# Two layers of a hybrid trunk on one core: gate slabs, turned norm factors, ada folds and two small operations put elsewhere

## The chip, the core and the metric

The program runs on one core of a Trainium2 chip. The core has engines that run side by side, each through its own list of instructions in order: TensorE (PE in the profile: matrix products and transpositions into PSUM), VectorE (DVE), ScalarE (ACT) and GpSimd (POOL) for elementwise work, and SyncE (SP), which issues the loads and stores. An instruction whose operands are not ready holds up all that stand behind it on its engine. The metric is the device time of one execution in microseconds; lower is better.

## The reference

Two layers over 512 latent tokens (x) and 256 context tokens (ctx), 1024 channels, float32. The second layer ("last") needs of the context only keys and values. Per layer, cut to what matters:

```python
mx = silu(c) @ w_ada + b_ada            # "ada rows": 6 shifts, scales and gates; mc likewise from c_ctx
hx = rmsnorm(x, norm1_g) * (1 + ax1) + sx1
p  = hx @ w_in                          # columns: conv GLU (a, g) | q | k | v | merge gates
z  = a * sigmoid(g);  y_conv = silu(layernorm(depthwise_conv31(z))) @ w_conv_out
q, k = rope(rmsnorm(q)), rope(rmsnorm(k))
w  = softmax(q0 k0') - lam * softmax(q1 k1')     # 8 heads, two maps each
o  = rmsnorm(w @ v) * (1 - lam_init);   y_attn = o @ w_attn_out
x += gx1 * ((g_conv * y_conv + g_attn * y_attn) @ w_out)
x += gx2 * relu(rmsnorm(x, norm2_g) * (1 + ax2) + sx2 @ w_mlp1)**2 @ w_mlp2
```

The hidden layer of the last line has 4096 channels. The output is x.

## The kernel before

Activations stand channel by channel: 128 channels on the partitions, 8 groups of channels, tokens along the free dimension. X holds the residual stream of 768 tokens (latent 0 to 511, context 512 to 767).

Each float32 product is made of three: every operand is a high part plus a low part, and TensorE does high x high (L109), high x low (L110), low x high (L111). Weights come as slabs of 1024 x 256 (`load_slab`): a load on SP into a "raw" buffer, then in two halves of 128 x 1024 the high part by a ScalarE copy (L76) and the low part by a subtraction (L77) on VectorE or GpSimd. A state entry "behind" makes the two steps of a slab be issued after a named instruction, "turn" does so for the second half alone. The order on each engine is set once, when the program is built, by a scheduler that simulates it; within a layer the steps run as generators which are merged by given costs.

A layer goes through these stages.

- Norm 1 in groups of 256 tokens (`norm_mod`): squares on ScalarE are summed by VectorE into acc (L354), TensorE sums over channels (nc_n, L327), VectorE scales (ms_n), GpSimd raises to -1/2, VectorE multiplies the identity by each factor (dg_n, L312), TensorE spreads the factors (nb_n, L316), and VectorE, ScalarE and GpSimd make the high and low parts (h1h and h1l, for norm 2 h2h and h2l). In the first layer's feed-forward part the norm of the second layer runs with the last additions to X, and the second layer's first q/k slab (wqk) and value slab (wv) are made ready there (`v_first`).
- Attention, head by head: q and k are normed and turned by GpSimd's rotary work (rqk, rw, ra, rb, dup) and transposed (qkT). Scores S, weights e, their transpositions wT with parts wth and wtl, outputs av, copied out by ScalarE (uo). The factor of each head's norm is gathered in rsall. During the last head the conv projections run: ca, then cg, whose sigmoid sg (L510) multiplies z.
- Mixing: the 31 taps of the depthwise convolution on VectorE (cacc, L963), spread over TensorE's gate products gt (slabs wg, half 1 for attention, half 0 for the convolution, four each), the turned factors (`spill_rstd`: rsT, L818, stored and loaded back spread over partitions as arb), the products of attention outputs with them (ar, L990), then ya (attention branch; its operand's parts are named h1l too), the layer norm of the convolution (tot, ln), yc (convolution branch) and the output projection o.
- Feed-forward in four chunks of 1024 hidden channels: f, then r, which is added to X (L1158). Meanwhile the first layer computes the second one's ada rows (`ada_rows`): 48 loads of half slabs, ScalarE and VectorE multiply and add (adaac, L276, L279), every second one is transposed and reduced into a column of adp (L289, L290), and after every 16 a TensorE product folds the partitions (adaps, L252). One step is taken behind each block of hidden channels (`ada_step`); what is left is drained ahead of the last chunk's r.

## Time and profile before

| what | us |
|---|---|
| median of 3 runs | 2350.78 (2348.27 to 2351.1) |
| the profiled execution | 2350.59, span 2348.8 |
| TensorE busy | 2275.5 |
| VectorE, ScalarE, GpSimd busy | 1491.8, 997.2, 685.5 |
| mean granted TensorE clock | 0.991 |

A row of the timeline gives the start, the time from the start of the first to the end of the last of its instructions, engine, line, operation, output and inputs, size and count; in brackets the idle time of the engine before it and what ended that. A row of the list of waits gives the total, the number of times and the longest. Windows show the busy time of each engine in a stretch and the clock that TensorE was granted there.

### The profile page before, as it was taken

How to read it: one execution, taken by the hardware profiler on the slowest of the kernel's cores; microseconds unless marked ns; L12 is line 12 of the kernel's file. 1: busy time of each engine (PE TensorE's matmuls, PEld its weight loads, DVE VectorE, ACT ScalarE, POOL GpSimd, SP SyncE). 2: the span in 40 equal slices, each digit the busy share in tenths (PEclk: the TensorE clock that was granted, in tenths of full speed). 3: DMA queues.
4: the chain of work that ended last, by engine and by line, in shares of the span. 5: the costliest groups of instructions: out<-in, count | busy, mean ns of one | idle time of the engine just before them, and what ended most of it. 6: DMA issues, size and time to landing. Idle time of an engine off the chain costs nothing.

```text
span 2348.8 us, 36385 instructions
## 1 busy us (share of the span) xinstructions
PE 2275.5 (97%) x14626; PEld 2039.2 (87%) x14626; DVE 1491.8 (64%) x2587; ACT 997.2 (42%) x1965; POOL 685.5 (29%) x790
## 2 busy tenths in 40 slices
PE   8999999999999999999999998999999999999999
PEld 6999998888878988888888998999877779888887
DVE  6777776699657455565656467767759966433332
ACT  5556654522333353342514345655642334432432
POOL 1866754100000133232323266757610000000000
PEclk9999999999999999999999999999999999999999
DMA  9211111143535123434343311111114324223222
GB/s 315 58 44 30 45 44 45 46 160 126 180 117 167 59 81 110 133 110 133 108 135 112 105 46 57 44 44 44 61 59 141 112 90 126 90 90 100 98 90 72
DMA packets 222570, 224.76 MB, mean 96 GB/s; under 512 B 6256, under 2 KB 212544, under 8 KB 222272
## 3 DMA queue, kind: packets, MB, share of 16 engines
q1 hardware_dynamic: 222400, 222.43, 29.5%
q8 instruction: 115, 1.88, 0.3%
q14 instruction: 55, 0.45, 0.1%
HBM read 208.73 MB, written 13.67 MB: 95 GB/s over the span
## 4 chain that ended last, share of the span: by engine, by line
PE 81%; DVE 9%; POOL 4%; ACT 3%; DMA 2%; issue 1%; ACTq 0%; SPq 0%; POOLq 0%; DVEq 0%
PE r L109 6%; PE r L111 6%; PE r L110 6%; PE f L110 6%; PE f L109 6%; PE f L111 6%; PE gt L109 3%; PE gt L111 3%; PE gt L110 3%; PE qk L109 2%; PE qk L110 2%; PE qk L111 2%; PE o L109 2%; PE o L110 2%; PE o L111 2%
## 5 line engine op out<-in xcount | busy, mean ns | idle before, releaser
L110 PE MATMUL f<-h2l,h_w 128*128 128x512 f32 (+1 forms) x832 | 284.6, 343 | 1.3 <-POOL h2l L77 1.3
L109 PE MATMUL f<-h2h,h_w 128*128 128x512 f32 (+1 forms) x832 | 282.8, 343 | 2.2 <-ACT h2h L76 1.7
L109 PE MATMUL r<-fh,h_w 128*128 128x512 f32 (+1 forms) x832 | 282.9, 341 | 0.0
L111 PE MATMUL f<-h2h,l_w 128*128 128x512 f32 (+1 forms) x832 | 282.9, 342 | 0.0
L110 PE MATMUL r<-fl,h_w 128*128 128x512 f32 (+1 forms) x832 | 282.9, 340 | 0.0
L111 PE MATMUL r<-fh,l_w 128*128 128x512 f32 (+1 forms) x832 | 282.8, 340 | 0.0
L77 POOL TENSOR_TENSOR l_w<-r_w,h_w 128x1024 fp32r<-128x1024 f32 x64 | 156.9, 2473 | 340.0 <-ACT h_w L76 340.0
L76 ACT ACTIVATE h_w<-r_w 128x1024 fp32r<-128x1024 f32 x128 | 128.6, 1052 | 255.9 <-PE r L110 117.2
L963 DVE SCALAR_TENSOR_TENSOR cacc<-z,cols,cacc 128x783 f32<-128x783 f32 (+1 forms) x240 | 201.4, 889 | 0.4
L279 DVE SCALAR_TENSOR_TENSOR adaac<-ar,cvec,adaac 128x256 f32<-128x256 f32 x336 | 164.9, 553 | 42.8 <-DMA ar<-in_w_ada_dram 23.0
L1158 DVE SCALAR_TENSOR_TENSOR X<-r,ad,X 128x512 f32<-128x512 f32 (+1 forms) x104 | 65.1, 626 | 189.8 <-PE r L111 189.4
L109 PE MATMUL qk<-h_wqk,h1h 128*128 128x256 f32 x640 | 182.6, 288 | 2.1 <-ACT rw L558 1.1
L110 PE MATMUL qk<-l_wqk,h1h 128*128 128x256 f32 x640 | 180.1, 284 | 0.0
L111 PE MATMUL qk<-h_wqk,h1l 128*128 128x256 f32 x640 | 176.3, 284 | 0.2 <-POOL h1l L77 0.2
L110 PEld LDWEIGHTS f<-h2l,h_w 128*128 128x128 f32 x832 | 159.0, 191 | 20.2 <-POOL h2l L77 2.4
L109 PEld LDWEIGHTS f<-h2h,h_w 128*128 128x128 f32 x832 | 158.1, 191 | 20.9 <-ACT h2h L76 2.3
L111 PEld LDWEIGHTS f<-h2h,l_w 128*128 128x128 f32 x832 | 158.8, 191 | 17.6
L111 PEld LDWEIGHTS r<-fh,l_w 128*128 128x128 f32 x832 | 157.7, 190 | 17.7
L110 PEld LDWEIGHTS r<-fl,h_w 128*128 128x128 f32 x832 | 157.8, 190 | 17.4
L109 PEld LDWEIGHTS r<-fh,h_w 128*128 128x128 f32 x832 | 157.7, 190 | 17.3
L730 DVE TENSOR_REDUCE st<-S 128x1 f32<-128x768 f32 (+1 forms) x160 | 134.4, 845 | 57.4 <-PE S L728 56.1
L1239 DVE TENSOR_TENSOR fl<-fr,fh 128x512 fp32r<-128x512 f32 (+1 forms) x104 | 71.0, 688 | 132.4 <-ACT fr L1238 132.1
(255 smaller groups left out, 6298.0 us busy)
## 6 DMA issues: line engine op xcount, KB each, us to landing
r_w<-in_w_mlp_dram SPq DMA_DIRECT2D x64, 1024.0 KB, 5.3
ada<-in_w_ada_dram SPq DMA_DIRECT2D x24, 1024.0 KB, 5.5
ar<-in_w_ada_dram SPq DMA_DIRECT2D x48, 512.0 KB, 3.6
r_wqk<-in_w_in_dram SPq DMA_DIRECT2D x32, 512.0 KB, 5.1
r_wg<-in_w_in_dram SPq DMA_DIRECT2D x16, 1024.0 KB, 5.8
r_wv<-in_w_in_dram SPq DMA_DIRECT2D x8, 1024.0 KB, 5.3
r_wao<-in_w_attn_out_dram SPq DMA_DIRECT2D x8, 1024.0 KB, 4.8
r_wo<-in_w_out_dram SPq DMA_DIRECT2D x8, 1024.0 KB, 8.8
```

Source lines behind the costliest of these rows:

```text
L76: nc.scalar.activation(out=hi, in_=src, func=AF.Copy)
L77: return (lo_eng or nc.vector).tensor_tensor(out=lo, in0=src, in1=f32(hi), op=ALU.subtract)
L109: nc.tensor.matmul(ps, sh, mh, start=first, stop=False)
L110: nc.tensor.matmul(ps, sh, ml, start=False, stop=False)
L111: nc.tensor.matmul(ps, sl, mh, start=False, stop=last)
L279: nc.vector.scalar_tensor_tensor(out=a[:, q], in0=r[:, j], scalar=cvec[:, k, q : q + 1], in1=a[:, q], op0=ALU.mult, op1=ALU.add)
L730: nc.vector.tensor_reduce(out=st[:, m : m + 1], in_=S[:, :nkey], axis=AX.X, op=ALU.max, negate=True)
L963: nc.vector.scalar_tensor_tensor(out=ca[cc][:, :CV], in0=zt[cc][:, t : t + CV], scalar=wcol, in1=ca[cc][:, :CV], op0=ALU.mult, op1=ALU.add)
L1158: state["done"] = nc.vector.scalar_tensor_tensor(out=X[:, mb, g], in0=ps[:, :W], scalar=gate[:, s, mb : mb + 1], in1=X[:, mb, g], op0=ALU. ...
L1239: state["done"] = nc.vector.tensor_tensor(out=fl[mb][:, g], in0=r[:, :W], in1=f32(fh[mb][:, g]), op=ALU.subtract).ins
```

## The change

It does four things.

1. `ada_rows` yields once more before each fold, so that a fold and all that comes after it are taken one step later.
2. `rstd_bcast` can multiply the identity on ScalarE. Norm 2 of the first layer does so for tokens 256 to 511.
3. In both layers the first gate slab (half 1, slab 0) is split behind the sigmoid of the conv gate block that was issued last before it. The second gate slab (1, 1) is taken after the last head's merge and split behind the last head's copy uo. The turned factors (`spill_rstd`) are taken after the issue of slab (1, 2), in a PSUM buffer of another pool.
4. The second half of layer 1's first value slab is issued behind the last sum of squares instead of behind the last low part of the norm, and its low part is made by VectorE, the first half's still by GpSimd.

```diff
@@ -291,6 +291,7 @@
                     out=part[:, :, 4 * (s % 8) : 4 * (s % 8) + 4].rearrange("p c n -> p n c"),
                     in_=b.rearrange("p (n c r) -> p n c r", n=4, c=4), axis=AX.X, op=ALU.add)
                 if s % 8 == 7:
+                    yield
                     fold(s - 7)
 
     def ada_gain(L, which, ks=slice(0, KT)):
@@ -302,21 +303,24 @@
                 op0=ALU.add, op1=ALU.mult)
 
 
-    def rstd_bcast(colsum, n, scale, name):
+    def rstd_bcast(colsum, n, scale, name, scalar=False):
 
         ms = spool.tile([P, 8], F32, tag="ms", name=f"ms_{name}")
         nc.vector.tensor_scalar(ms[:, :n], colsum, scale, EPS, ALU.mult, ALU.add)
         nc.gpsimd.tensor_tensor(out=ms[:, :n], in0=ms[:, :n], in1=mhalf[:, :n], op=ALU.pow)
         dg = spool.tile([P, 4, P], F32, tag="dg", name=f"dg_{name}", bufs=1)
         for t in range(n):
-            nc.vector.tensor_scalar(dg[:, t, :], ident, ms[:, t : t + 1], None, ALU.mult)
+            if scalar:
+                nc.scalar.activation(out=dg[:, t, :], in_=ident, func=AF.Copy, scale=ms[:, t : t + 1])
+            else:
+                nc.vector.tensor_scalar(dg[:, t, :], ident, ms[:, t : t + 1], None, ALU.mult)
         return dg
 
     def bcast(ps, dg, n):
         nc.tensor.matmul(ps[:, : n * P], ones, dg[:, :n, :].rearrange("p t d -> p (t d)"),
                          start=True, stop=True)
 
-    def norm_mod(xt, acc, toks, s, A, sh, hh, hl, name):
+    def norm_mod(xt, acc, toks, s, A, sh, hh, hl, name, scalar=False):
 
         mi = state["mi"]
         n = (toks.stop - toks.start) // P
@@ -326,7 +330,7 @@
             lo = toks.start + t * P
             nc.tensor.matmul(ps[:, t : t + 1], acc[:, lo : lo + P], ones[:, 0:1],
                              start=True, stop=True)
-        dg = rstd_bcast(ps[:, :n], n, 1.0 / D, name)
+        dg = rstd_bcast(ps[:, :n], n, 1.0 / D, name, scalar)
         rb = mi(f"nb_{name}")
         bcast(rb, dg, n)
         for k in range(KT):
@@ -351,7 +355,8 @@
             sq = state["xp"].tile([P, 512], F32, tag="u", bufs=3, name=f"nsq_{name}_{k}")
             W = toks.stop - toks.start
             nc.scalar.activation(out=sq[:, :W], in_=xt[:, k, toks], func=AF.Square)
-            nc.vector.tensor_tensor(out=acc[:, toks], in0=acc[:, toks], in1=sq[:, :W], op=ALU.add)
+            state["sum"] = nc.vector.tensor_tensor(out=acc[:, toks], in0=acc[:, toks],
+                                                   in1=sq[:, :W], op=ALU.add).ins
 
 
     xpool = tc.tile_pool(name="xpool0", bufs=1, side="right", reuse_waits="tile")
@@ -507,7 +512,8 @@
                     fm_block(ps[:, :W], w, m * P, lambda k: (hh[:, k], hl[:, k]), g)
                     z0 = PAD if g is LAT else ZC
                     sgt = ap.tile([P, 768], F32, tag="e0", name=f"sg{i}_{cc}_{g.start}", bufs=2)
-                    nc.scalar.activation(out=sgt[:, :W], in_=ps[:, :W], func=AF.Sigmoid)
+                    gated[:] = [nc.scalar.activation(out=sgt[:, :W], in_=ps[:, :W],
+                                                     func=AF.Sigmoid).ins]
                     zz = zt[cc][:, z0 : z0 + W]
                     nc.vector.tensor_tensor(out=zz, in0=zz, in1=sgt[:, :W], op=ALU.mult)
                     if m == 0 and g is LAT and s == 0:
@@ -515,6 +521,7 @@
                     yield 5.3 if g is LAT else 2.7
 
         wg = {}
+        gated, ended = [], []
 
         def gate_slab(half, s, lo_eng=None):
             wg[half, s] = load_slab(rows(wi, G_OFF + half * D + 256 * s, 256),
@@ -524,9 +531,10 @@
 
             g = conv_g(1)
             yield next(g)
+            state["behind"] = tuple(gated)
             gate_slab(1, 0, nc.gpsimd)
+            state["behind"] = ()
             yield from g
-            gate_slab(1, 1)
 
 
         sqs = [ap.tile([P, 4, QK + 1], F32, tag=f"sqe{n}", name=f"sqe{i}_{n}", bufs=1) for n in range(2)]
@@ -770,7 +778,8 @@
                 sq = ap.tile([P, 256], F32, tag="osq", name=f"osq{i}_{h}_{u}", bufs=1)
                 nc.scalar.activation(out=sq, in_=av[:, :256], func=AF.Square)
                 uo = ap.tile([P, 256], F32, tag="uo", name=f"uo{i}_{h}_{u}")
-                nc.scalar.activation(out=uo, in_=av[:, :256], func=AF.Copy, scale=L["ag"])
+                ended[:] = [nc.scalar.activation(out=uo, in_=av[:, :256], func=AF.Copy,
+                                                 scale=L["ag"]).ins]
                 nc.sync.dma_start(at_d[i][h, :, 256 * u : 256 * u + 256], uo)
                 d["sq"], d["av"] = sq, av
 
@@ -814,7 +823,7 @@
         def spill_rstd():
 
             n = H * qt_n
-            ps = mm_tile(f"rsT{i}")
+            ps = state["mi"](f"rsT{i}")
             nc.tensor.transpose(ps[:n, :P], rsall, ident)
             row = spool.tile([P, 4, P], F32, tag="dg", name=f"rst{i}", bufs=1)[:, 0]
             nc.vector.tensor_copy(row[:n], ps[:n, :P])
@@ -923,7 +932,9 @@
             if h == H - 1:
                 main = chain_(main, rest_of(carry))
             merge(main, chain_(*fill), fc / att_cost)
-        drain(spill_rstd())
+        state["behind"] = tuple(ended)
+        gate_slab(1, 1)
+        state["behind"] = ()
         for pl in (psx, pspool, apool):
             pl.__exit__(None, None, None)
 
@@ -997,6 +1008,8 @@
             for s in range(4):
                 if (half, s) not in wg:
                     gate_slab(half, s)
+                if (half, s) == (1, 2):
+                    drain(spill_rstd())
                 if half == 0 and s == 3:
                     for hg in branch[:4]:
                         branch_load(*hg)
@@ -1198,7 +1211,8 @@
         h2l = hpool.tile([P, KT, NT], F32R, tag="hl", name=f"h2l{i}")
 
         def norm2(g):
-            norm_mod(X, acc, g, int(g.start >= SEQ), L["A2"], sh2, h2h, h2l, f"n2_{i}_{g.start}")
+            norm_mod(X, acc, g, int(g.start >= SEQ), L["A2"], sh2, h2h, h2l, f"n2_{i}_{g.start}",
+                     scalar=not last and g is halves[1])
 
         w1 = {}
 
@@ -1266,8 +1280,8 @@
 
             def v_first():
 
-                state["turn"] = state["n1"]
-                first["v"] = v_slab(i + 1, 0, nc.gpsimd)
+                state["turn"] = state["sum"]
+                first["v"] = v_slab(i + 1, 0, (nc.gpsimd, None))
                 state["turn"] = None
 
             def qk_start():
```

The order that the scheduler makes of it, at three places. First, VectorE around the second fold, in the third chunk of the first layer's feed-forward part. Before:

```order
L289 STREAM_TRANSPOSE adat1_15_12266<-adaac1_15_12117 128x512
L279 SCALAR_TENSOR_TENSOR adaac1_16_12275<-ar1_32_12166,cvec_330,adaac1_16_12275 128x256 x2
L290 TENSOR_REDUCE adp1_8_11245<-adat1_15_12266 128x4x4
L279 SCALAR_TENSOR_TENSOR adaac1_16_12275<-ar1_32_12166,cvec_330,adaac1_16_12275 128x256 x4
L254 TENSOR_TENSOR ad1_9372<-adaps1_8_12269,cols1_9344 128x8x2x2
L1239 TENSOR_TENSOR fl0_2_7_11771<-fr0_2_7_0_12311,fh0_2_7_11770 128x512
L1239 TENSOR_TENSOR fl0_2_6_11769<-fr0_2_6_512_12341,fh0_2_6_11768 128x256
L1239 TENSOR_TENSOR fl0_2_7_11771<-fr0_2_7_512_12371,fh0_2_7_11770 128x256
L1158 SCALAR_TENSOR_TENSOR X1_8448<-r0_2_0_0_12384,ad0_141,X1_8448 128x512
```

With the change:

```order
L1253 TENSOR_TENSOR fl0_2_7_11761<-fr0_2_7_512_12351,fh0_2_7_11760 128x256
L1171 SCALAR_TENSOR_TENSOR X1_8448<-r0_2_0_0_12364,ad0_141,X1_8448 128x512
L289 STREAM_TRANSPOSE adat1_15_12390<-adaac1_15_12147 128x512
L290 TENSOR_REDUCE adp1_8_11271<-adat1_15_12390 128x4x4
L1171 SCALAR_TENSOR_TENSOR X1_8448<-r0_2_1_0_12393,ad0_141,X1_8448 128x512
L279 SCALAR_TENSOR_TENSOR adaac1_16_12425<-ar1_32_12264,cvec_330,adaac1_16_12425 128x256 x2
L254 TENSOR_TENSOR ad1_9372<-adaps1_8_12419,cols1_9344 128x8x2x2
```

The reduce into adp1_8 stood behind two accumulations for the next row, and the fold's result (ad1) was taken three rows later, before the last low parts of the hidden channels. Now the reduce stands behind the chunk's first addition to X, and no accumulation stands between its transposition and it.

Second, GpSimd at the start of layer 1's attention. Before:

```order
L77 TENSOR_TENSOR h1l_1_9380<-nu_n1_1_256_5_14228,h1h_1_9379 128x256
L77 TENSOR_TENSOR h1l_1_9380<-nu_n1_1_256_7_14237,h1h_1_9379 128x256
L77 TENSOR_TENSOR l_wv1_0_14370<-r_wv1_0_14367,h_wv1_0_14369 128x1024
L309 TENSOR_TENSOR ms_n1_1_512_14478<-ms_n1_1_512_14478,mhalf_79 128x2
L534 MEMSET sqe1_0_14535 128x4
L534 MEMSET sqe1_1_14536 128x4
L564 TENSOR_TENSOR rqk1_0_14541<-rqk1_0_14541,mhalf_79 128x4 x3
```

With the change:

```order
L77 TENSOR_TENSOR h1l_1_9380<-nu_n1_1_256_5_14228,h1h_1_9379 128x256
L77 TENSOR_TENSOR h1l_1_9380<-nu_n1_1_256_7_14237,h1h_1_9379 128x256
L542 MEMSET sqe1_0_14535 128x4
L542 MEMSET sqe1_1_14536 128x4
L310 TENSOR_TENSOR ms_n1_1_512_14478<-ms_n1_1_512_14478,mhalf_79 128x2
L572 TENSOR_TENSOR rqk1_0_14541<-rqk1_0_14541,mhalf_79 128x4 x3
```

The subtraction of the second half of the value slab (l_wv1_0) left GpSimd between the norm's low parts and the power ms_n1_1_512; VectorE does it, right ahead of ms_n1_1_512. The two memsets now stand ahead of the power.

Third, ScalarE at the end of layer 1's attention. Before:

```order
L510 ACTIVATE sg1_2_0_18923<-cg1_2_0_18898 128x512
L76 ACTIVATE wth1_7_1_1_18645<-wT1_7_3_1_18835 128x3x128
L76 ACTIVATE h_wg1_1_1_18964<-r_wg1_1_1_18962 128x1024 x2
L510 ACTIVATE sg1_3_0_18959<-cg1_3_0_18934 128x512
L771 ACTIVATE osq1_7_1_18860<-av1_7_1_18841 128x256
L773 ACTIVATE uo1_7_1_18862<-av1_7_1_18841,ag1_9370 128x256
```

With the change:

```order
L515 ACTIVATE sg1_2_0_18923<-cg1_2_0_18898 128x512
L76 ACTIVATE h_wg1_1_0_18928<-r_wg1_1_0_18926 128x1024 x2
L76 ACTIVATE wth1_7_1_1_18645<-wT1_7_3_1_18835 128x3x128
L515 ACTIVATE sg1_3_0_18959<-cg1_3_0_18934 128x512
L779 ACTIVATE osq1_7_1_18860<-av1_7_1_18841 128x256
L781 ACTIVATE uo1_7_1_18862<-av1_7_1_18841,ag1_9370 128x256
L76 ACTIVATE h_wg1_1_1_18964<-r_wg1_1_1_18962 128x1024 x2
```

The copies of slab (1, 0), which stood twelve rows above the first row shown, now come behind the third sigmoid (sg1_2_0), and those of slab (1, 1) went from ahead of the last sigmoid to behind uo1_7_1. On TensorE the first two gate blocks gt1_1_0 and gt1_1_1 now stand between the last head's products and around its sums, and rsT1 behind them. On SP the load of the fifth gate slab (r_wg1_0_0) now stands ahead of the loads of the third to the eighth turned factor (arb).

## The prediction

> **What bounds the kernel now.** I read the page first, then TensorE's waits, then windows and the timeline at each place that the change touches.
>
> ```profile
> PE 2275.5 (97%) x14626; PEld 2039.2 (87%) x14626; DVE 1491.8 (64%) x2587; ACT 997.2 (42%) x1965; POOL 685.5 (29%) x790
> PEclk9999999999999999999999999999999999999999
> ```
>
> TensorE is busy for 2275.5 of 2348.8 us. The change alters none of its matmuls, so only two things can be won: its 73.3 us of idle time, and time in which its clock is below full speed. The 40 slices of 59 us hide the second. The waits that the change aims at:
>
> ```profile
> PE nc_n L327 <- DVE acc L354: 2.7, 2, 2.5
> PE adaps L252 <- DVE adp L290: 1.9, 1, 1.9
> PE nb_n L316 <- DVE dg_n L312: 1.8, 1, 1.8
> ```
>
> The last number is the longest one. Right behind each of these three, short windows (columns: window, us, then busy time and count of PE, PEld, DVE, ACT, POOL, then granted clock, DMA share, GB/s) show:
>
> ```profile
> 830.00:834.00 4.00, 4.00 (x23) 4.00 (x22) 3.26 (x9) 2.99 (x8) 0.74 (x1) 0.57 0.82 261
> 834.00:840.00 6.00, 6.00 (x52) 6.00 (x51) 3.84 (x10) 5.11 (x16) 2.27 (x3) 1.00 0.00 0
> 1165.00:1169.00 4.00, 4.00 (x23) 4.00 (x23) 1.45 (x4) 1.22 (x3) 0.00 (x0) 0.59 0.43 131
> 1390.00:1394.00 4.00, 4.00 (x23) 3.97 (x21) 1.90 (x6) 0.93 (x3) 3.17 (x6) 0.57 0.00 0
> ```
>
> TensorE looks busy, yet did 23 matmuls in 4 us where 52 in 6 us (0.115 us each) is normal: 11.7 too few, 1.35 us. So each such stall costs about 1.4 us more than its wait, and both go if the stall goes. [...]
>
> **The change part by part.**
>
> *Fold of the ada rows (L290, L252).* The reduce that TensorE waits for stood behind an accumulation that started late:
>
> ```profile
> 1161.72 0.91 ACT L276 ACTIVATE adaac<-ar,cvec 128x256 f32<-128x256 f32 x2 [5.28 <-DMA ar<-in_w_ada_dram]
> 1162.27 0.88 DVE L279 SCALAR_TENSOR_TENSOR adaac<-ar,cvec,adaac 128x256 f32<-128x256 f32 x2 [2.65 <-ACT adaac L276]
> 1163.07 0.68 DVE L290 TENSOR_REDUCE adp<-adat 128x16 f32<-128x512 f32 x1
> ```
>
> In the new order the reduce follows the first residual addition directly, and the fold comes 28 matmuls after that addition's operand is done: 24 of 512 columns and 4 of 256, at 0.23 and 0.115, make 6 us. VectorE needs for that addition, a transposition and the reduce about 0.7 each, 2.1 in all. The wait of 1.9 goes, and 1.4 of clock: **3.3 us**. What is late next: the last pair of rows is accumulated in the first residual additions of the last feed-forward slab (ten more operations of 0.4 to 0.7 us, 5 us in all), where VectorE itself waits for TensorE before most additions, as in this row of that place, so nobody waits for it:
>
> ```profile
> 1314.78 0.48 DVE L1158 SCALAR_TENSOR_TENSOR X<-r,ad,X 128x256 f32<-128x256 f32 x1 [2.40 <-PE r L111]
> ```
>
> On SP each weight slab now goes ahead of an ada load, which helps TensorE. Ends: 1.9 (clock lost anyway) and 3.5.
>
> *Norm2 factors, tokens 256 to 511 (L312).*
>
> ```profile
> 822.72 2.01 ACT L76 ACTIVATE h_w<-r_w 128x1024 fp32r<-128x1024 f32 x2 [3.44 <-PE o L110]
> 824.19 4.72 POOL L77 TENSOR_TENSOR l_w<-r_w,h_w 128x1024 fp32r<-128x1024 f32 x2
> 824.26 4.73 DVE L312 TENSOR_SCALAR dg_n<-cst,ms_n 128x128 f32<-128x128 f32 x2 [0.88 <-POOL ms_n L309]
> 827.22 0.38 ACT L1236 ACTIVATE fr<-f 128x256 f32<-128x256 f32 x1 [2.50 <-PE f L111]
> 845.78 0.48 DVE L312 TENSOR_SCALAR dg_n<-cst,ms_n 128x128 f32<-128x128 f32 x2 [0.60 <-POOL ms_n L309]
> ```
>
> The same pair takes 0.48 us alone and 4.73 beside GpSimd's two subtractions: VectorE ends when GpSimd does. ScalarE is free from 824.73 to 827.22 and needs about 0.8 for two (an estimate from 0.38 for 128x256), so the factors are ready near 825.6; today TensorE arrives 1.8 before that wait ends at about 829.1, so at 827.3, and in the new order 5 matmuls later, 827.9. Gain 1.8 + 1.4 = **3.2 us**. That ScalarE is held up like VectorE is the risk, though its copies run beside GpSimd at their usual 1.0 each. What follows moves too: VectorE's normalising steps start about 1 to 1.6 earlier, since GpSimd holds them until 828.9, while the matmuls that read their result come 3.2 earlier. But 59 matmuls lie between the broadcast and the block that reads the later parts, 6.8 us at the normal rate, so I count no new wait. Ends 1.0 and 3.3.
>
> *First value slab of layer 1.* GpSimd's second subtraction no longer stands in the last sums:
>
> ```profile
> 1385.22 2.55 POOL L77 TENSOR_TENSOR l_wv<-r_wv,h_wv 128x1024 fp32r<-128x1024 f32 x1
> 1385.65 2.93 DVE L354 TENSOR_TENSOR acc<-acc,nsq_sr 128x256 f32<-128x256 f32 x2
> 1390.78 0.75 DVE L563 TENSOR_REDUCE rqk<-sqe 128x4 f32<-128x260 f32 x2
> 1391.27 2.96 POOL L564 TENSOR_TENSOR rqk<-rqk,mhalf 128x4 f32<-128x4 f32 x3 [0.83 <-DVE rqk L563]
> 1409.03 1.60 POOL L582 TENSOR_TENSOR dup<-ra,rb 128x256 f32<-128x256 f32 x2
> 1410.00 0.66 PE L596 MATMUL qkT<-cst,dup 128*128 128x128 f32 x4 [0.54 <-POOL dup L582]
> 1412.27 1.23 DVE L77 TENSOR_TENSOR l_wqk<-r_wqk,h_wqk 128x1024 fp32r<-128x1024 f32 x1
> ```
>
> Two sums of 0.4 end near 1386.5 instead of 1388.6, so the wait falls from 2.5 to 0.5 and its clock loss goes: TensorE is 3.4 earlier. But it does not keep this. The rotary work on GpSimd runs without a pause from 1391.27 to 1410.6 and starts behind VectorE's factors, which now stand behind the subtraction of 1.23 us: that ends at 1387.7, the factors at 1389.2, the first reduce 1.6 earlier than 1390.78. The third query transposition, which waits 0.54 today, then waits 0.54 + 3.4 - 1.6 = 2.3. So 1.6 is kept, less a clock loss of 1.4 that a gap of 2.3 brings in perhaps half of its positions: **1.0 us**. Ends 0 and 3.4.
>
> *Gate slab, layer 0.*
>
> ```profile
> 467.38 5.75 POOL L77 TENSOR_TENSOR l_wg<-r_wg,h_wg 128x1024 fp32r<-128x1024 f32 x2
> 467.81 3.06 DVE L963 SCALAR_TENSOR_TENSOR cacc<-z,cols,cacc 128x783 f32<-128x783 f32 x1
> 475.82 0.41 DVE L77 TENSOR_TENSOR wtl<-wT,wth 128x256 fp32r<-128x256 f32 x1
> 476.29 0.39 PE L110 MATMUL av<-wtl,vh 128*128 128x256 f32 x1 [1.24 <-DVE wtl L77]
> ```
>
> The tap takes 3.06 instead of 1.02 and the low part of the weights comes 1.24 late. The pair moves some 7 us back, behind the sigmoid, into taps for which nobody waits soon: **1.2 us**. Ends -1 and 2.6.
>
> *Mixing, layer 1: gate slabs and turned factors.*
>
> ```profile
> 1740.00:1780.00 40.00, 31.16 (x143) 25.29 (x142) 29.43 (x45) 13.90 (x27) 7.34 (x6) 0.83 0.22 72
> 1780.00:1800.00 20.00, 20.00 (x90) 16.55 (x89) 20.00 (x31) 5.19 (x7) 0.00 (x0) 1.00 0.67 226
> 1745.25 4.69 POOL L77 TENSOR_TENSOR l_wg<-r_wg,h_wg 128x1024 fp32r<-128x1024 f32 x2 [9.58 <-ACT h_wg L76]
> 1747.72 3.04 DVE L743 SCALAR_TENSOR_TENSOR e<-e,st,e 128x768 f32<-128x768 f32 x1
> 1772.34 0.96 PE L781 MATMUL av<-cst,osq 128*128 128x1 f32 x4 [1.82 <-ACT uo L773]
> 1774.79 0.40 PE L818 MATMUL rsT<-cst,rsall 128*32 128x128 f32 x1 [1.49 <-POOL rsall L788]
> 1870.74 0.50 PE L110 MATMUL ya<-h1l,h_wao 128*128 128x512 f32 x1 [0.58 <-DVE h1l L77]
> 1877.19 1.13 PE L1035 MATMUL ln<-tot,cst 128*128 128x512 f32 x2 [0.72 <-DVE tot L1032]
> 1913.78 0.50 PE L118 MATMUL yc<-ch,h_wco 128*128 128x512 f32 x1 [0.94 <-ACT ch L1070]
> ```
>
> Here most idle time lies: 8.84 of 40 us, and a clock of 0.83. The waits of 1.82 and 1.49 get gate matmuls in front of them, the scores' VectorE step loses its GpSimd neighbour (2.0 of its 3.04), and with the clock TensorE should reach the third gate block some 6.5 us earlier. But from 1780 VectorE has no idle time, and TensorE meets it again at 1870 (h1l, 0.58) and 1877 (tot, 0.72). VectorE's work is the same; it starts its taps about 2 us earlier, idles less, but the GpSimd pair now falls into them and holds two taps for some 2 us each. I make VectorE 1 to 3 us earlier. In its new order the tail's sum comes ahead of the fifth h1l part, 1.3 later. So the wait at 1870 grows from 0.58 to 4 or 5 us, and the gain is VectorE's, less a clock loss: **1.0 us**. Ends -4 (a second clock loss, and the normalising step that now waits 1.4 longer before yc) and 6.5.
>
> Sum: 3.3 + 3.2 + 1.0 + 1.2 + 1.0 = 9.7. The profiled execution took 2350.59 (its span of 2348.8 and 1.8 around it), so 2340.9 there; the median of the runs is 2350.78, 0.2 more: **2341 us**.
>
> **The rivals.**
> *TensorE keeps the mixing.* If VectorE gains as TensorE does (its 7.3 us beside GpSimd before 1780 speak for it, the full 20.00 against), that term is 6.5 and the first value slab's up to 2: 2341 - 6.5 = 2335.
> *Half clock without the stalls.* If the slow windows don't come from the gaps, only waits go: 1.9 + 1.8 + 1.6 + 1.2 + 1 = 7.5, less the waits given back: near 2344. [...] All three windows standing right behind a gap speak against it.
> *Given back.* TensorE's earlier arrival meets producers that don't move (rotary work, VectorE's taps, h2 parts of tokens 256 to 511): of 9.7 some 3 remain, 2348: no change that can be told.
> *Slower: the load queue in the mixing.*
>
> ```profile
> 1789.31 2.85 SPq L988 DMA_DIRECT2D arb<-rs_d  x3
> 1794.77 0.38 SPq L90 DMA_DIRECT2D r_wg<-in_w_in_dram  x1
> ```
>
> SP issues in order. The next gate slab, which waits for a buffer that VectorE frees, now stands ahead of four factor loads that VectorE multiplies with between its taps. If that wait comes due late, VectorE stands at the product until the load has come, and taps, h1l and ya all slide with it. It decides once VectorE stands for more than the 8.7 us won elsewhere; at 11 us the time is 2350.8 - 8.7 + 11 = 2353. Against it: between the subtraction that frees the buffer and the first product behind that load lie eleven taps of 0.7, two products of 0.7 and two subtractions of 1.2, 11.5 us in all.
>
> **How the numbers follow.** Chances: forecast 0.62 (2337 to 2345), TensorE keeps the mixing 0.11, half clock stays 0.08, given back 0.13, slower 0.06. About 0.2%, 4.7 us, is what a measurement here can tell from no change. Faster is the first three, 0.81, less 0.02 for their upper edges: 0.79; same 0.15; slower 0.06. The range takes in the mixing won below and most of the given-back case above: 2333 to 2348.
>
> **What would show it.** In the new profile the waits of adaps, nb_n (tokens 256 to 511) and nc_n should be below 0.6 us and the clock near 1.0 behind them. dg_n on ScalarE should take about 0.4 each. The third qkT should wait about 2 us for dup, the first or second ya 4 to 5 us for h1l. Wrong would be: dg_n slow on ScalarE, a factor product waiting for its load, a new gap at the first residual additions of the last slab, or ya without a longer wait (then the gain is larger).

## The result and the profile after

| | us | ratio to before, 95% interval |
|---|---|---|
| before | 2350.78 | |
| the change, first time | 2338.96 (2335.27 to 2340.07) | 0.9948 (0.9937 to 0.9959) |
| the change, a second time beside the experiments | 2341.51 (2336.16 to 2343.04) | 0.9954 (0.9938 to 0.9970) |

The change is faster by 10.8 to 12.2 us (0.46 to 0.52%). 2341 had been forecast. The profiled execution took 2339.04, span 2337.3, clock 0.994 where it was 0.991. The first part of its page:

```profile
PE 2272.6 (97%) x14626; PEld 2036.2 (87%) x14626; DVE 1488.6 (64%) x2586; ACT 996.0 (43%) x1967; POOL 681.8 (29%) x789
PEclk9999999999999999999999999999999999999999
```

TensorE's idle time fell from 73.3 to 64.7 us, 8.6; the other 2.9 is its busy time, which contains the half-clock stretches. Of the three waits that the change aims at, the list of TensorE's waits (total, times, longest) has one left (nc_n). Three others have grown, those of rsT (1.5 before), of yc for ch (0.9) and of ya for h1l (0.6), and that of ya for h1h has fallen from 3.4:

```profile
PE rsT L827 <- POOL rsall L797: 3.0, 1, 3.0
PE yc L118 <- ACT ch L1083: 2.3, 1, 2.3
PE ya L110 <- DVE h1l L77: 2.1, 1, 2.1
PE ya L109 <- ACT h1h L76: 1.6, 1, 1.6
PE nc_n L331 <- DVE acc L358: 0.5, 1, 0.5
```

adaps and nb_n have no row any more. The timeline at the places of the first three parts:

```profile
821.73 0.68 ACT L314 ACTIVATE dg_n<-cst,ms_n 128x128 f32<-128x128 f32 x2
825.54 1.26 DVE L338 SCALAR_TENSOR_TENSOR nu_n<-X,A,nb_n 128x256 f32<-128x256 f32 x3 [5.06 <-PE nb_n L320]
1166.14 0.69 DVE L290 TENSOR_REDUCE adp<-adat 128x16 f32<-128x512 f32 x1
1170.65 0.27 PE L252 MATMUL adaps<-adp,fold 128*32 128x32 f32 x8
1376.98 1.22 DVE L77 TENSOR_TENSOR l_wv<-r_wv,h_wv 128x1024 fp32r<-128x1024 f32 x1
1377.21 0.58 PE L331 MATMUL nc_n<-cst,acc 128*128 128x1 f32 x4 [0.55 <-DVE acc L358]
1380.04 2.96 POOL L572 TENSOR_TENSOR rqk<-rqk,mhalf 128x4 f32<-128x4 f32 x3 [0.93 <-DVE rqk L571]
1391.45 0.39 PE L110 MATMUL kc<-h1l,h_wqk 128*128 128x256 f32 x1 [0.43 <-POOL h1l L77]
1398.37 0.65 PE L604 MATMUL qkT<-cst,dup 128*128 128x128 f32 x4 [1.24 <-POOL dup L590]
```

The two factors take 0.68 us on ScalarE beside GpSimd's subtractions, where the same pair took 4.73 on VectorE; now VectorE waits for TensorE (5.06) and not the other way round. The reduce of the ada rows ends 3.8 us before TensorE folds (6 less 2.1 had been worked out). The wait for the sums is 0.55, the third qkT waits 1.24, and between them there is a new wait of 0.43 for a low part of the norm (h1l). Behind the second norm the clock is now full (windows; columns as in the prediction), where before had 0.57:

```profile
826.50:829.90 3.40, 3.40 (x31) 3.40 (x30) 3.20 (x8) 3.40 (x12) 1.60 (x2) 1.00 0.79 237
```

In layer 1's mixing the gate slab and the turned factors moved as forecast, and the waits moved with them:

```profile
1780.00:1800.00 20.00, 20.00 (x90) 16.57 (x89) 19.10 (x27) 6.12 (x8) 0.00 (x0) 1.00 0.72 241
1800.00:1857.00 57.00, 54.89 (x243) 45.02 (x241) 57.00 (x80) 20.57 (x27) 0.00 (x0) 1.00 0.38 123
1768.08 2.74 POOL L797 TENSOR_TENSOR rsall<-rsall,mhalf 128x2 f32<-128x2 f32 x1 [12.09 <-ACT rsall L794]
1770.87 0.28 PE L827 MATMUL rsT<-cst,rsall 128*32 128x128 f32 x1 [3.04 <-POOL rsall L797]
1857.04 0.61 PE L110 MATMUL ya<-h1l,h_wao 128*128 128x512 f32 x1 [2.15 <-DVE h1l L77]
1902.25 0.51 PE L118 MATMUL yc<-ch,h_wco 128*128 128x512 f32 x1 [2.30 <-ACT ch L1083]
```

From 1800 to 1857 VectorE has not one idle moment (57.00 of 57.00), and TensorE meets it at ya (0.58 before, 2.15 now), then ScalarE at yc (0.94 before, 2.30 now).

### The profile page after: what moved, and what is told of

It reads as the page before. It is cut to its first block, busy times and chain, and to the rows that moved or that the text cites. A ratio compares the mean times of both kernels' runs of the same rounds, so it can differ in the third digit from the quotient of the medians.

```text
span 2337.3 us, 36377 instructions
## 1 busy us (share of the span) xinstructions
PE 2272.6 (97%) x14626; PEld 2036.2 (87%) x14626; DVE 1488.6 (64%) x2586; ACT 996.0 (43%) x1967; POOL 681.8 (29%) x789
## 4 chain that ended last, share of the span: by engine, by line
PE 78%; DVE 11%; POOL 4%; ACT 3%; DMA 2%; issue 2%; SPq 0%; POOLq 0%; DVEq 0%; ACTq 0%
PE r L109 6%; PE r L111 6%; PE r L110 6%; PE f L109 6%; PE f L110 6%; PE f L111 6%; DVE cacc L974 3%; PE qk L109 2%; PE qk L110 2%; PE qk L111 2%; PE gt L109 2%; PE gt L110 2%; PE gt L111 2%; PE o L109 2%; PE o L110 2%
## 5 line engine op out<-in xcount | busy, mean ns | idle before, releaser
L76 ACT ACTIVATE h_w<-r_w 128x1024 fp32r<-128x1024 f32 x128 | 128.6, 1052 | 225.4 <-PE r L110 117.2
L974 DVE SCALAR_TENSOR_TENSOR cacc<-z,cols,cacc 128x783 f32<-128x783 f32 (+1 forms) x240 | 207.8, 917 | 0.3
L1253 DVE TENSOR_TENSOR fl<-fr,fh 128x512 fp32r<-128x512 f32 (+1 forms) x104 | 77.3, 746 | 155.7 <-ACT fr L1252 155.5
L279 DVE SCALAR_TENSOR_TENSOR adaac<-ar,cvec,adaac 128x256 f32<-128x256 f32 x336 | 156.5, 529 | 20.4 <-ACT adaac L276 15.5
```

The lines of the kernel that those rows point to most:

```text
L76: nc.scalar.activation(out=hi, in_=src, func=AF.Copy)
L279: nc.vector.scalar_tensor_tensor(out=a[:, q], in0=r[:, j], scalar=cvec[:, k, q : q + 1], in1=a[:, q], op0=ALU.mult, op1=ALU.add)
L974: nc.vector.scalar_tensor_tensor(out=ca[cc][:, :CV], in0=zt[cc][:, t : t + CV], scalar=wcol, in1=ca[cc][:, :CV], op0=ALU.mult, op1=ALU.add)
L1253: state["done"] = nc.vector.tensor_tensor(out=fl[mb][:, g], in0=r[:, :W], in1=f32(fh[mb][:, g]), op=ALU.subtract).ins
```

## Where the time went, stage by stage

Single runs of one kernel lie up to 13 us apart (before: 2344.19 to 2356.96), so timed medians tell parts of 2 us only roughly. The traces do better: between fixed points of TensorE's list most stages repeat to 0.1 us. The table holds, for each profiled kernel of this study, the time in us between the first starts of the groups named (cg and ya of layer 0; ln, the second layer-norm group behind ya; nb, the first spread of norm 2 of layer 0; r, the first block of its feed-forward; f3, its third f chunk; nc4 and nc5, the first two sums groups of layer 1's first norm; kcT, layer 1's first key transposition; cg to o of layer 1):

```
              cg-ya    ya-ln   nb-r   f3-nc4   nc5-kcT   cg-o (layer 1)
before        194.50   36.42   89.99  255.66   37.86     198.02
the change    193.03   31.83   86.44  252.58   35.37     197.69
again         193.07   31.89   86.44  252.49   35.39     197.75
e1_fold       194.50   33.79   90.05  252.17   37.86     198.20
e2_norm2      194.50   34.45   86.45  254.61   37.85     200.39
e3_value      194.48   34.00   88.51  255.87   35.38     198.27
e4_gates      195.00   32.41   88.53  255.99   37.85     198.10
e5 not l0     194.50   31.61   86.45  252.17   35.40     197.64
e6 not l1     193.07   31.11   86.46  252.51   35.41     197.93
e9 not norm2  193.03   31.75   88.51  252.87   35.38     197.94
e11 three     194.49   36.23   86.45  252.70   35.38     198.11
e7 one tap    193.07   34.85   86.46  252.17   35.40     193.10
e8 queue      193.09   30.45   86.44  252.17   35.36     197.17
e10           193.05   30.00   86.45  252.65   35.39     198.33
```

Most columns have two levels, and with two exceptions, which come below, an edit moves only its own column. ya-ln scatters, and in the last column the levels overlap (197.17 to 198.10 with the part, 197.93 to 198.33 without). The difference of the means is what a part is worth: layer 0's gate part 194.5 - 193.06 = 1.4 up to ya and 34.4 - 32.3 = 2.1 up to ln; the second norm's factors 89.1 - 86.45 = 2.7; the fold 255.53 - 252.45 = 3.1; the value slab 37.86 - 35.38 = 2.5; layer 1's gate part 198.14 - 197.72 = 0.4. (Left out are e4's 195.00, which holds a half-clock stretch in the scores, and of the last column e2 and e7; e8 and e10 are left out of the second column.) The 2.1 is the difference of two groups of six that overlap (31.61 to 36.42 without the part, 31.11 to 34.85 with it) and is sure to about 2 us only. The sum is 12.2, and the two timings gave 12.2 and 10.8; so close a match owes something to chance. The stages that are not listed hold next to nothing of the change: from the start to cg it is 436 to 441 in all kernels, from kcT to the last head's key work in layer 1 (kcD) 290.8 to 293.2. These two and ya-ln hold most of the scatter between the traces.

## Experiment 1: each part alone

The edits, each on the kernel before. The fold (e1):

```diff
                 if s % 8 == 7:
+                    yield
                     fold(s - 7)
```

The factors (e2):

```diff
+            if scalar:
+                nc.scalar.activation(out=dg[:, t, :], in_=ident, func=AF.Copy, scale=ms[:, t : t + 1])
+            else:
                 nc.vector.tensor_scalar(dg[:, t, :], ident, ms[:, t : t + 1], None, ALU.mult)
```

The value slab (e3):

```diff
-                state["turn"] = state["n1"]
-                first["v"] = v_slab(i + 1, 0, nc.gpsimd)
+                state["turn"] = state["sum"]
+                first["v"] = v_slab(i + 1, 0, (nc.gpsimd, None))
```

The gate slabs and turned factors (e4) are the remaining lines of the change, in both layers. And the changed kernel once more (after2), beside them.

> The kernel before with the deferred fold alone (one more step of the background generator before the modulation columns are folded), nothing else changed. Theory (as in the forecast, and as the two traces have it, where TensorE's lead grows from 6.5 to 9.5 us over this place): the adaps wait of the norm goes, with it the half-clock window behind it; TensorE is about 3.1 us earlier from there on and keeps it, since the later waits of the kernel are short: time 3.3 us less, about 2347.5. If the window does not come from the stall, only the wait goes: 1.9 less, 2348.9. Rival: given back in the value slab or in the mixing of layer 1, where VectorE sets the end: 0 to 1 less, about 2350.

> The kernel before with the diagonal factors of the second norm (tokens 256 to 511, layer 0) made on ScalarE alone. Theory: the nb_n wait goes, and the half-clock window at about 819 us of the span with it: 3.2 us less, about 2347.6, each factor on ScalarE 0.3 to 0.4 us. If the window does not hang on the stall: 1.8 less, 2349.0. Rival: ScalarE's next work comes later by the four factors, and the feed-forward's first activations wait: 0 to 1 less, about 2350.

> The kernel before with the first value slab's low part on VectorE alone, begun behind the last sums. The forecast gave this part 1.0 us (a new wait of the third query transposition, 2.3 us, and half a clock loss). The traces of before and after give TensorE a lead that grows by 2.5 us here, with that wait at 1.24 us and no half-clock window. Theory now: 2.5 less, about 2348.3, the third qkT waiting 1.2 us for dup. If the forecast's term was right and the rest came from the parts ahead of it: 1.0 less, 2349.8. Rival: the rotary work on GpSimd sets the end whatever TensorE does, 0 less.

> The kernel before with the gate slabs queued behind the sigmoid and behind the last head's copy, and the norm factors turned later, in both layers; the other three parts left out. The forecast gave 1.2 for layer 0 and 1.0 for layer 1: 2.2 less, about 2348.6. Theory now: in layer 0 the lead is swallowed at the attention's output product, where before waits 3.4 us and after 1.6 us for the same load's product on ScalarE and goes on at the same moment of the span (650.1 and 650.2); only a half-clock window of 6.8 us that before has there (worth up to 2.7 us) may or may not go. So 0.3 to 0.5 less by layer 1 alone, about 2350.4, and up to 3 less, 2347.6, if that window goes. Rival: the gate parts carry most of the gain that the forecast gave to others, 5 less, 2346.

> The changed kernel once more, unaltered, so that it, the parts and the kernel before are timed side by side. The four parts one by one gave 2.4, 0.9, 1.7 and 1.8 less by their medians, 6.8 in all; the whole gave 11.8 less. Theory now: a half-clock stretch of TensorE always begins at a point of a grid of 3.413 us that lies anew in every run, and follows a piece of that grid in which TensorE stood still for more than about 1.9 us; so the profile of before, which had such stretches behind all three removed stalls, showed more than the mean run loses, and the mean gain of the whole should lie nearer the sum of the parts: 8 less, 2342.5. Rival: the parts help each other (one part alone lets the planner set a worse order in the mixing of layer 1), 12 less, 2338.7.

| | median us | ratio, 95% | difference |
|---|---|---|---|
| e1 fold | 2348.07 | 0.9991 (0.9979 to 1.0002) | -2.1 (-4.9 to 0.5) |
| e2 factors | 2349.59 | 1.0002 (0.9991 to 1.0013) | 0.5 (-2.1 to 3.1) |
| e3 value slab | 2348.87 | 0.9996 (0.9987 to 1.0004) | -0.9 (-3.1 to 0.9) |
| e4 gates | 2348.71 | 0.9988 (0.9978 to 0.9998) | -2.8 (-5.2 to -0.5) |
| after2 | 2341.51 | 0.9954 (0.9938 to 0.9970) | -10.8 (-14.6 to -7.1) |

(The difference is the ratio applied to 2350.5.) The four ratios add up to -5.3, the whole is -10.8, and the intervals are too wide to say that the parts fall short of the whole. e2's interval excludes the 3.2 that were expected of it, and e4's the lowest case (0.3); e1's and e3's decide between none of their theories. For the whole the two theories said 2342.5 and 2338.7, and 2341.51 does not tell them apart. In the traces each edit does in its column what it does in the whole: e1 255.66 to 252.17, e3 37.86 to 35.38, e2 89.1 to 86.45. So the parts don't lose in their own places what they win.

The factors alone are the clear case of a loss elsewhere. They change nothing in layer 1, but the scheduler that sets the orders simulates the whole program, and with this edit it put several copies, subtractions, taps and products of layer 1's last head and mixing in another order. There cg-o is 200.39 where the other kernels with an unchanged layer 1 have 198.1. Among these is e11 (below), which has the same edit together with two others, and in whose layer 1 VectorE and ScalarE keep the order of before; so it is the order, and not the factors as such. The timelines of e1 and then of e2, at the first yc:

```profile
1910.01 0.50 PE L118 MATMUL yc<-ch,h_wco 128*128 128x512 f32 x1 [0.94 <-ACT ch L1071]
```

```profile
1909.68 0.50 PE L118 MATMUL yc<-ch,h_wco 128*128 128x512 f32 x1 [2.30 <-ACT ch L1073]
```

In e2 the wait is 1.36 longer, and a stretch at half clock follows it at 1910.1 (worth up to 1.7, half of its 3.41). 2.7 won and 2.3 lost fits the small change that was measured. The whole change has the same wait of 2.30, but there TensorE reaches layer 1's first ya 4.1 us earlier behind cg (128.6 against 132.7), which pays for it.

## Experiment 2: the change with one part taken back

Layer 0's gate part as before (e5), or layer 1's (e6): the lines of that part stand under a condition on `last`, the flag of the second layer; the line shown is e5's.

```diff
-            state["behind"] = tuple(gated)
+            state["behind"] = tuple(gated) if last else ()
```

The factors taken back (e9), and both gate parts taken back (e11, the kernel before with the edits of e1, e2 and e3):

```diff
-            norm_mod(X, acc, g, int(g.start >= SEQ), L["A2"], sh2, h2h, h2l, f"n2_{i}_{g.start}",
-                     scalar=not last and g is halves[1])
+            norm_mod(X, acc, g, int(g.start >= SEQ), L["A2"], sh2, h2h, h2l, f"n2_{i}_{g.start}")
```

> The changed kernel with layer 0's gate slab and factors as before, layer 1's as changed. Theory (what layer 0 gains is swallowed at the attention's output product, which waits for the last head's load): the same time as the changed kernel within 0.5, that wait about 1 us shorter than in the changed kernel's trace. Rival (the forecast's term): 1.2 slower; and if the shorter wait decides whether a half-clock stretch follows, up to 2.6 slower.

> The changed kernel with layer 1's gate slab and factors as before, layer 0's as changed. Theory: VectorE sets the end of the mixing, TensorE's lead of 8 us there is given back at ya, ln and yc: 0 to 0.5 slower than the changed kernel, and as the waits of 3.0, 2.15 and 2.3 us at rsT, ya and yc shrink, perhaps faster by 1. Rival (the forecast's term): 1.0 slower. Rival (TensorE keeps its lead): 6.5 slower.

> The changed kernel with the second norm's factors back on VectorE, the other three parts as changed. That part alone, put on the kernel before, gained 0.9 by the medians and nothing by the ratio, though its trace shows TensorE 3.2 us earlier behind the removed wait; its planner set the order in layer 1's mixing anew, and TensorE lost 2.0 of it there. Theory: in the changed kernel that loss is there either way (yc waits 2.3 us for ch), so the part is worth its wait and its share of half-clock stretches: 1.8 + 0.5 x 1.5, time about 2.5 more than the changed kernel, 2342 to 2343. Rival: the part is worth nothing, 0 to 0.7 more.

> The kernel before with the deferred fold, the ScalarE factors and the value slab's part, and with both layers' gate slabs and turned factors left as before. Theory: the gate parts are swallowed in both layers (attention's output product in layer 0, VectorE in layer 1), so this kernel has the whole gain within 1: about 2340. Rival (the forecast's terms): 2.2 less gain, 2342 to 2343; and by the gate parts' own run, which gave 1.8 less by medians, 2341.5.

| | median us | ratio, 95% | difference to before |
|---|---|---|---|
| e5 without layer 0's gates | 2341.85 | 0.9964 (0.9951 to 0.9976) | -8.5 (-11.5 to -5.6) |
| e6 without layer 1's gates | 2338.60 | 0.9949 (0.9933 to 0.9964) | -12.0 (-15.7 to -8.5) |
| e9 without the factors | 2341.50 | 0.9963 (0.9949 to 0.9976) | -8.7 (-12.0 to -5.6) |
| e11 without either layer's gates | 2342.51 | 0.9966 (0.9953 to 0.9979) | -8.0 (-11.0 to -4.9) |

The whole lies at -10.8 and -12.2. e6: layer 1's gate part is worth nothing that can be told (0.4 in the table). By the ratios, e9, e11 and e5 are some 2 to 4 us slower than the whole, but their intervals overlap the whole's, so the traces have to decide. e9: nb-r is 88.51 instead of 86.45, so in the whole the factors are worth their 2.1 without the half-clock stretch, and not nothing. e11 and e5: here a theory drawn from the first two traces fell. It had been that layer 0's lead is swallowed at ya, since before and after wait there for the same load and go on at the same moment (650.23 and 650.09). But these two executions were 3.2 us apart at cg by what happened at their start. Counted from cg, TensorE comes to this wait at 209.5 in all six kernels with layer 0 as before, and at 208.1 in five of the six with the gate part (e4, with its half-clock stretch, at 210.0). The load follows: its issue on SP ends at 203.7 on average without the part and at 202.1 with it, and VectorE starts the first product with it at 210.6 and at 208.8. So the load gains 1.8, about as much as TensorE, the lead is kept, and from cg to ln the six with the part take 225.7 on average where the others take 228.9.

The wait for that load is 1.36, 2.05, 2.24, 2.82, 3.19 and 3.41 without the part and 0.86, 1.50, 1.57, 1.65, 2.16 and 3.07 with it. Half-clock stretches follow in five of the first six and in one of the others, which makes the second column: 34.4 and 32.3. That the part shortens this wait as well is likely by these numbers and not certain, as the two rows overlap. What the gate slabs and the turned factors each do in a layer was not separated.

## Experiment 3: who sets the end of layer 1's mixing

One VectorE tap per group of channels taken out of layer 1 (e7); the output lacks that tap's share:

```diff
-                for t in range(TAPS):
+                for t in range(TAPS - 1 if last else TAPS):
```

> The changed kernel with one of the 31 taps of layer 1's depthwise convolution left out (four VectorE steps of about 0.7 us each, 2.8 us in all, so the output lacks that tap's share); layer 0 is whole. Theory (VectorE sets the end of layer 1's mixing): VectorE reaches the last parts of h1l and the norm of the convolution 2.8 us earlier; the wait of ya for h1l, 2.2 to 2.4 us in the two traces of the changed kernel, is gone or under 1, and the time falls by 2 to 3, to about 2337. Rival (TensorE or the normalising chain on ScalarE sets the end): the wait of yc for ch grows by as much as ya's falls, less than 0.7 us in the time.

Measured: 2334.89 us, ratio 0.9935 (0.9922 to 0.9947); the changed kernel had 0.9948 and 0.9954. The intervals overlap, but in the trace cg-o falls from 197.7 to 193.10, 4.6 for 2.8 us of VectorE work (2 to 3 were expected in the time), and no other kernel is below 197.17; ya-ln is by chance at its worst there, with a wait of 3.07, or the time would be lower still. e7's timeline:

```profile
1856.36 0.50 PE L110 MATMUL ya<-h1l,h_wao 128*128 128x512 f32 x1 [0.85 <-DVE h1l L77]
1898.33 0.50 PE L118 MATMUL yc<-ch,h_wco 128*128 128x512 f32 x1 [0.94 <-ACT ch L1083]
```

The wait at ya is 0.85 instead of 2.15, as VectorE as the bound demands, and yc's did not take it over: it fell too, by 1.36. With this edit the order around yc came out otherwise, with yc's wait as in before, so this part of the 4.6 can't be put down to the tap. The half-clock stretch behind ya, which the changed kernel has at 1857.3, is gone as well. So at ya VectorE sets the end, and most of what TensorE wins ahead of the taps is waited for there: with layer 1's part it comes to ya 4.1 us earlier, and 0.4 is left at o.

## Experiment 4: the load behind two slabs

In layer 0 the last head's load (0.25 MB) stood on SP behind two slabs of 1 MB. The changed kernel:

```profile
636.30 0.38 SPq L81 DMA_DIRECT2D ada<-in_w_ada_dram  x1
638.55 0.53 SPq L90 DMA_DIRECT2D r_wao<-in_w_attn_out_dram  x1
639.75 2.42 SPq L996 DMA_DIRECT2D ar<-at_d  x1
648.68 0.69 DVE L1001 TENSOR_TENSOR ar<-ar,arb 128x512 f32<-128x512 f32 x1 [3.22 <-DMA ar<-at_d]
650.09 0.50 PE L109 MATMUL ya<-h1h,h_wao 128*128 128x256 f32 x2 [1.57 <-ACT h1h L76]
```

The product that needs it starts 8.9 us after SP begins to issue the load; the issue itself takes 2.42 of them. The edit (e8), shown for the weights; the modulation slab gets the same with s > 0, and state["ar"] is the load:

```diff
+            with ExitStack() as queue:
+                if s > 1 and not last:
+                    queue.enter_context(tc.issue_after(state["ar"]))
                 w = load_slab(rows(w_attn_out[i], 256 * s, 256), f"wao{i}_{s}")
```

e10 is e8 with e6's condition in layer 1.

> The changed kernel with one thing moved on SP's queue in layer 0: the last head's attention load (0.25 MB) is issued ahead of a modulation slab and a slab of the output weights (1 MB each). Theory: the wait of the attention's output product for that head, 1.6 to 3.4 us in six traces with a mean of 2.4, falls below 1 us, and the half-clock stretch that followed it in four of the six goes: 2 to 4 less than the changed kernel. Rival: the weights' slab that now comes later stalls the next block of that product, or the products before it: 0, or slower by 1 to 3.

> The changed kernel with the last head's load moved ahead on SP's queue in layer 0 and with layer 1's gate slab and factors as before, the two edits that took nothing or gained. Theory: their effects add, 2 to 4 less than the changed kernel by the queue and 0 to 1 by layer 1, where yc waits 0.9 instead of 2.3 us: 2335 to 2337. Rival: VectorE sets the end of the mixing in both, and only the queue's gain is left: 2337 to 2338.

Measured: e8 2337.26, ratio 0.9937 (0.9921 to 0.9952), and e10 2335.50, 0.9939 (0.9924 to 0.9955), beside 2341.51 and 0.9954 of the changed kernel. In e8:

```profile
641.94 0.37 SPq L996 DMA_DIRECT2D ar<-at_d  x1
642.41 0.41 SPq L81 DMA_DIRECT2D ada<-in_w_ada_dram  x1
644.85 0.69 DVE L1002 TENSOR_TENSOR ar<-ar,arb 128x512 f32<-128x512 f32 x1
640.00:660.00 20.00, 19.81 (x110) 16.82 (x109) 17.20 (x31) 6.20 (x10) 0.00 (x0) 1.00 0.54 177
```

The issue now begins later (641.94) but takes 0.37, the product starts 2.9 us after its beginning, and TensorE is busy for 19.81 of 20 us at full clock. ya-ln is 30.45 and 30.00 instead of 32.3, the mean with the gate part: 2.1 us, near the lower end of what was expected (1.6 against the changed kernel's own two traces). Both point to a version some 2 to 4 us faster than the change; by the timed runs alone, whose intervals overlap, that is not certain, and e10 is not told apart from e8 (its cg-o is 198.33, e8's 197.17).

## The clock: what the fourteen traces say together

The forecast's price of a stall (its wait and 1.4 of clock) came from three windows of one run. Which stalls pay it showed only in the set. The trace's clock records give every stretch at half speed with its start. Within each of the fourteen runs the starts lie whole multiples of 3.4133 us apart, to within 0.004 (in before nine starts, the first at 383.21 us of the span and the last 575 multiples later, at 2345.87); where this grid lies differs from run to run. Counting TensorE's gaps (those above 0.1 us, by the ends of matmuls that the profile gives) in each piece of the grid, for all pieces at full clock from 41 to 2300 us:

```
idle time in the piece    followed by full clock    by half clock
under 1.4 us              8991                      1
1.4 to 1.8                36                        9
1.8 to 2.0                2                         25
2.0 to 3.3                0                         58
```

In these counts the clock goes with the idle time within one piece: half clock followed 58 of 58 pieces with 2.0 us or more and 9 of 45 with 1.4 to 1.8. The length of a gap alone does not tell the cases apart, as two runs at the same place (layer 0's ya) show, windows laid on the pieces. e1_fold, a wait of 2.05 within one piece:

```profile
645.82:649.23 3.41, 1.36 (x11) 1.15 (x10) 1.75 (x3) 0.63 (x1) 0.00 (x0) 1.00 0.04 14
649.23:652.64 3.41, 3.41 (x18) 3.41 (x17) 0.66 (x2) 0.16 (x1) 0.00 (x0) 0.50 0.00 0
```

e4_gates, a wait of 2.16 over two pieces, 0.44 and 1.72:

```profile
643.16:646.58 3.42, 2.98 (x25) 2.77 (x24) 0.00 (x0) 0.00 (x0) 0.00 (x0) 1.00 0.37 117
646.58:649.99 3.41, 1.69 (x14) 1.69 (x15) 1.98 (x3) 0.63 (x1) 0.00 (x0) 1.00 0.00 0
649.99:653.40 3.41, 3.41 (x18) 2.58 (x17) 2.62 (x5) 2.76 (x4) 0.00 (x0) 1.00 0.00 0
```

The longer gap cost less: the piece behind it has a clock of 1.00, that of e1_fold 0.50. The same shows in the table of stages: the unchanged second norm has a wait of 1.84 in all five traces, and nb-r is 88.5 in three of them and 90.0 in the two in which a half-clock stretch follows. 1.5 is thus the price of one stretch there. Of the pieces that were themselves at half clock, 37 of the 39 with 0.4 us or more of idle time were followed by another, none of the 89 with under 0.2.

## Why the prediction was right

2341 against 2338.96 and 2341.51. The mechanism held: the three stalls and the wait at av went, with the half clock that had followed some of them, and VectorE took back most of what TensorE won in layer 1's mixing. That the sum came so near owes something to luck, as errors of both signs offset each other. Point by point, by its own steps:

- **Fold, 3.3.** Measured 3.1. Right: the wait went, nothing else came. One of the four kernels without this part (e2, 254.61) has the wait, 2.38 there, without a half-clock stretch behind it.
- **Factors, 3.2.** 3.5 where the unchanged kernel has the half-clock stretch behind this wait (before, e1), 2.1 where it has not, 2.7 on average. The two on ScalarE took 0.34 each, as written (about 0.4). The step that was too sure is that the 1.4 of clock hangs on every such stall. A part of the kernel before's profile was chance: it had the stretch behind all three stalls.
- **First value slab, 1.0.** Mis-sized: 2.5. The first reduce behind the slab came 1.7 earlier (1.6 forecast) and TensorE's lead grew by 3.25 (3.4 forecast). But 0.43 of the lead went into the new wait for h1l, and GpSimd's chain from the reduce to dup took 0.4 less; so the third qkT waits 1.24, not 2.3. The granted clock behind it is 1.00 (1399.89 to 1403.30), so the clock loss that was taken off did not come either; that a gap of 2.3 brings it in half of its positions was an estimate that no run shows.
- **Gate slab, layer 0, 1.2.** Right up to where it was worked out (1.4), but the forecast looked no further than av. 175 us later TensorE waits for the last head's load, which the profile of before showed with 3.41 us, its longest wait for an operand made on the chip. The load comes earlier with the part by about as much as TensorE does, so the 1.4 is kept; on average the wait and the half clock behind it were shorter too, 2.1 more, of which part may be chance. That wait should have been in the list of places.
- **Mixing, layer 1, 1.0.** 0.4. The mechanism was right: VectorE sets the end. The size of the wait at ya was not (2.15 and 2.39 in place of 4 to 5): counted from cg, TensorE was 4.1 earlier at the third gate block, not 6.5, since of the two waits ahead of it that of 1.82 went but rsT's grew from 1.49 to 3.04. VectorE's last tap came 2.5 earlier, inside the 1 to 3 of the forecast. So TensorE went on 2.5 earlier behind the wait at ya, but a half-clock stretch came behind it, and the loss that the forecast kept as a lower end, the normalising chain that waits 1.4 longer before yc, came as well (2.30 against 0.94).
- **The rivals.** TensorE does not keep the mixing (e6, e7). Given back: the lead that TensorE brings to the rotary work grows there, and the lead that it brings to layer 1's mixing (11.2 us against before) is there at its end (11.5). The half clock without the stalls fell with the count above. The load queue of the mixing: from 1800 to 1857 VectorE is never idle, from 1780 to 1800 for 0.9 us, so no product waited for its factors for longer.

The sum of the measured terms is 12.2 where 9.7 was forecast; two terms were short by 1.5 and 2.3, three too large by 0.2 to 0.6.

## What to carry to other kernels

Where single runs scatter by more than the edit is worth, cut the traces of all variants at the same fixed points of the bounding engine: two levels in one column show what the medians cannot, and a column that scatters shows how far a mean may be trusted. Price a stall with its clock loss only as a chance (here the same wait of 1.84 us at the second norm was followed by half clock in two of five traces), and look along the whole list for the next wait that an earlier arrival meets, also hundreds of us later. In a program whose order is set by a simulation, an edit tested alone can lose its gain at a place that it does not touch, so take parts out of the whole as well as putting them in alone.

## What the runs showed of the hardware

- In the fourteen traces 58 of 58 pieces of 3.413 us at full clock in which TensorE stood idle for 2.0 us or more were followed by half clock; where the pieces begin differed from run to run, and with the same wait of 1.84 us the second norm's stage took 88.5 us in three runs and 90.0 in the two with a half-clock stretch.
- Beside GpSimd's subtractions of 128x1024, two VectorE products of 128x128 took 4.73 us (before; 0.48 without them), and on ScalarE the same two took 0.68 (the changed kernel).
- A load of 0.25 MB behind two of 1 MB was used 8.9 us after its issue began (6.5 after it ended; the changed kernel), ahead of them 2.9 (2.5; e8).
